# A gated linear attention layer: another order of its small steps, with its operand chains and state stores cut into parts

## The chip, the cores and the metric

The kernel runs on one core of a Trainium2 chip. Its engines work side by side, each through its own list of instructions in order: TensorE (PE, matrix products, with its weight loads listed as PEld), VectorE (DVE), ScalarE (ACT), GpSimd (POOL) and SyncE (SP, which here issues loads from memory). They wait for each other at semaphores. The metric is the device time of one execution in microseconds (us), the median of several runs.

## The reference

One inference step of a four-layer decoder, for one prompt of 256 rows and eight samples of 4 rows, with the same weights; the model width is 1024. The layers mix tokens by pooling, by windowed attention, by gated linear attention and by pooling again, and each is followed by a convolutional feed-forward part. The change touches the third layer's mixer alone. Per head (4 heads, keys of 128, values of 256) it computes

```python
log_a = log_sigmoid(gd @ w_gate_up + b_gate) / 16        # a gate for every key dimension
b = cumsum(log_a)                                        # within a chunk
o_inter = (q * exp(b)) @ S                               # what the state holds
att[t, s] = sum_k q[t, k] * k[s, k] * exp(b[t, k] - b[s, k])   # s <= t
o = o_inter + att @ v
S_new = exp(b_end) * S + (k * exp(b_end - b)).T @ v
o = rms_norm(o) * norm_gain
out = (o * silu(r)) @ w_out
```

The prompt begins with a state of zero; each sample brings a state of 4 x 128 x 256 and hands back a new one.

## The kernel before

**Products in parts.** Every large product is made of three products of rounded parts. A weight piece (4 blocks of 128 rows by 256 columns) is loaded to `raw`, ScalarE writes its rounded part `whi` (L345), VectorE the remainder `wlo` (L353), and `prod` (L414 to L416) sums high by high, high by low and low by high in PSUM. Pieces are split up to four ahead of their use. Six `raw` buffers hold loaded units (1 MB each); SP issues the loads in order (L324), each once its buffer is free.

**The order is written by hand.** `gla_steps` makes a dictionary of named steps and `GLA_ORDER` lists their names; the program is recorded in that order, so the list sets the order on every engine. A name such as `q1c` is a quarter of a projection (12 products for `q`, `k`, `r`, 16 row products for `v`); `w0a` is half of a quarter of the output product (24 products), and a `+` inserts a unit of the next layers' adaLN product (L534). The small steps between them are:

- `ga0` to `ga2`: the gates of a row tile. A product to PSUM (L1605), minimum and difference on VectorE (L1608, L1609), exponential and logarithm on ScalarE, a difference on POOL (L1612). `cu0` to `cu3`: the running sum of a head, as a product with a triangle (L1619, L1620).
- Attention inside a chunk of 128 rows is built in seven levels (halves of 64, 32, ... 1 rows) and a diagonal. `x`, `e` and `z` of a level make its operands: differences of `b` on POOL (L1652, L1653), the exponential on ScalarE (L1657), products with `k` and `q` on VectorE (L1659, L1660). `m0a`, `m0b` and so on multiply them on TensorE for the two row tiles (L1670) and put the result under a mask into `PT0`, `PT1` on VectorE (L1640). `xs5`, `xs6`, `ms5` to `ms7` do the same for the samples (`PTs`).
- `v0` to `v3`: values as rows. The last quarter also evacuates them: ScalarE copies, then a sum `vt` (L809) and a remainder `vs` (L1780) on VectorE.
- `ea`, `eb`, `ec`: the prompt's `K` and `Q` with their decay to the chunk's end; `es` the same for the samples; `ks`, `ps`: key rows and padded attention of the samples. `cr`, `kr`, `op`: attention across the two chunks, transposed keys, the prompt's output of a head.
- For the samples' states, per head: `up` pads the queries on POOL (`qp`, L1818, L1822), `kk` makes masked keys on POOL (`kp`, L1826; one buffer), `uo` multiplies the old state (L1838, L1840), `un` in four parts makes the new state (L1848, and L1851 on VectorE, in the `raw` buffer), whose last part also issues the store (L1854) from POOL. `sp0`, `sp1`: the prompt's new state (L1810, copied by L1811).
- `nq`, `ns`, `nr`, `nm`: squares, sums, roots and scaling of the norm; `og`: times the gate `r` (POOL, L1909), then rounded part and remainder (`gh`, `gl` for heads 0 and 1, `hh`, `hl` for heads 2 and 3).

**Buffers.** Results of the small products share two PSUM buffers (`aux`, tag `aux`) in turn: a product waits until the copy from the one before the last has ended. The projections have four (`mm`), one more (`acc`) holds sums. In SBUF the operands `X` of a level share two buffers (tag `D`), every third has its own (tag `K`).

## Time and profile before

| what | value |
|---|---|
| median of 3 runs | 1399.58 us (1395.9 to 1400.92) |
| the profiled execution | 1404.07 us, its span 1402.3 us |
| mean granted TensorE clock in it | 0.972 |
| TensorE busy | 1337.8 us (95% of the span) |
| VectorE, ScalarE, POOL busy | 850.7, 639.8, 200.2 us |
| gated layer's mixer, first projection to output product | 717.79 to 881.98 us from the span's start |

A row of the timeline gives the start, the duration, the engine, the line, the operation, the output and inputs with their sizes, and in brackets how long the engine had been idle and what ended that. Rows of waits give the waiting engine with its line, what it waited for, the total, the number of times and the longest. Rows of stretches give the busy time of each engine, the granted clock (1.00 is full speed) and the share of the DMA engines. A matrix product on 32-bit data that is not rounded has two records, so eight records are four products.

### The profile page before, as it was taken

The numbers are of one execution on the slowest core, as the hardware profiler recorded it, in microseconds if no ns is written. First come the engines' busy times: TensorE is split into PE (matmuls) and PEld (weight loads), VectorE is DVE, ScalarE is ACT, GpSimd is POOL, SyncE is SP. The second block draws the span as 40 slices with busy tenths as digits, with TensorE's granted clock in tenths as the row PEclk, the third lists the DMA queues.
The fourth block names the chain that finished last, engine by engine and source line by source line (L and its number), as shares of the span: only waits on it lengthen the run. The fifth ranks groups of instructions, "written<-read, shape, count | busy, mean of one in ns | idle before, by whom it ended". The sixth has DMA issues, their size and how long they took to land.

```text
span 1402.3 us, 25413 instructions
## 1 busy us (share of the span) xinstructions
PE 1337.8 (95%) x10075; PEld 1207.1 (86%) x10075; DVE 850.7 (61%) x1674; ACT 639.8 (46%) x1154; POOL 200.2 (14%) x501
## 2 busy tenths in 40 slices
PE   5899999999999999999998988999999999999998
PEld 2478889998887799899978875889999977999997
DVE  3476566556445776665565646586666466777654
ACT  3264344435434464444354435264444345545542
POOL 2211000002001111211033423031010021101100
PEclk9799999999999999999999998999999998999998
DMA  9997788658644787996493244797764576545520
GB/s 350 339 306 272 244 290 299 200 175 286 205 158 152 258 276 274 385 337 203 145 310 118 91 148 155 259 291 257 247 225 161 174 255 215 182 156 164 174 85 34
DMA packets 206231, 310.48 MB, mean 221 GB/s; under 512 B 7692, under 2 KB 186742, under 8 KB 196496
## 3 DMA queue, kind: packets, MB, share of 16 engines
q1 hardware_dynamic: 201296, 286.82, 61.2%
q0 software_dynamic: 4352, 21.50, 4.0%
q8 instruction: 79, 1.29, 0.4%
q10 hardware_dynamic: 464, 0.54, 0.1%
q14 instruction: 40, 0.33, 0.1%
HBM read 300.21 MB, written 19.76 MB: 228 GB/s over the span
## 4 chain that ended last, share of the span: by engine, by line
PE 84%; DVE 8%; ACT 3%; DMA 2%; issue 1%; POOL 1%; SPq 0%; DVEq 0%; ACTq 0%; POOLq 0%
PE mm L414 23%; PE mm L416 22%; PE mm L415 22%; PE adaps L534 4%; PE ps L410 2%; DVE ht L674 1%; DVE hl L710 1%; DVE wlo L353 1%; DMA own<-x_prompt 1%; PE mm L796 1%; PE sqps L596 1%; DMA raw<-w_ada 1%; PE mm L798 1%; PE mm L797 1%; ACT whi L345 1%
## 5 line engine op out<-in xcount | busy, mean ns | idle before, releaser
L414 PE MATMUL mm<-hh,whi 128*128 128x288 f32 x1720 | 517.8, 301 | 4.7 <-ACT hh L705 3.1
L416 PE MATMUL mm<-hh,wlo 128*128 128x288 f32 x1720 | 511.9, 298 | 2.7 <-DVE wlo L353 2.7
L415 PE MATMUL mm<-hl,whi 128*128 128x288 f32 x1720 | 512.5, 298 | 1.9 <-DVE hl L710 1.7
L345 ACT ACTIVATE whi<-raw 128x1024 fp32r<-128x1024 f32 (+2 forms) x335 | 342.7, 1029 | 308.8 <-PE mm L415 230.0
L353 DVE TENSOR_TENSOR wlo<-raw,whi 128x1024 fp32r<-128x1024 f32 (+2 forms) x335 | 394.7, 1195 | 145.2 <-ACT whi L345 144.9
L414 PEld LDWEIGHTS mm<-hh,whi 128*128 128x128 f32 x1720 | 326.5, 190 | 22.7 <-issue 11.2
L415 PEld LDWEIGHTS mm<-hl,whi 128*128 128x128 f32 x1720 | 326.6, 190 | 4.3 <-POOL hs L678 1.7
L416 PEld LDWEIGHTS mm<-hh,wlo 128*128 128x128 f32 x1720 | 326.4, 190 | 3.9 <-DVE wlo L353 3.6
L414 PE MATMUL mm<-ah,whi 128*128 128x288 f32 x704 | 208.5, 296 | 0.0
L416 PE MATMUL mm<-ah,wlo 128*128 128x288 f32 x704 | 208.0, 295 | 0.0
L415 PE MATMUL mm<-al,whi 128*128 128x288 f32 x704 | 206.9, 294 | 0.0
L415 PEld LDWEIGHTS mm<-al,whi 128*128 128x128 f32 x704 | 132.8, 189 | 0.0
L414 PEld LDWEIGHTS mm<-ah,whi 128*128 128x128 f32 x704 | 132.5, 188 | 0.0
L416 PEld LDWEIGHTS mm<-ah,wlo 128*128 128x128 f32 x704 | 132.3, 188 | 0.0
L853 DVE TENSOR_SCALAR c<-ext,vec 128x304 f32<-128x304 f32 x88 | 38.4, 436 | 122.7 <-ACT ext L850 120.2
L856 DVE SCALAR_TENSOR_TENSOR c<-ext,vec,c 128x304 f32<-128x304 f32 x176 | 94.4, 536 | 6.3
L534 PE MATMUL adaps<-raw,cT 128*32 128x512 f32 x736 | 94.2, 642 | 3.3 <-DMA raw<-w_ada 3.3
L862 POOL COPY convS<-ext 128x2 f32<-128x2 f32 x88 | 16.2, 184 | 470.4 <-ACT ext L849 470.3
L849 ACT ACTIVATE ext<-mm 128x256 f32<-128x256 f32 x88 | 33.9, 385 | 86.0 <-PE mm L416 85.9
L872 DVE TENSOR_TENSOR a<-ge,mm 128x256 f32<-128x256 f32 x88 | 36.7, 417 | 49.9 <-PE mm L416 46.4
L534 PEld LDWEIGHTS adaps<-raw,cT 128*32 128x32 f32 x736 | 21.0, 114 | 52.8 <-issue 40.5
L859 ACT ACTIVATE ge<-c 128x304 f32<-128x304 f32 x88 | 39.9, 458 | 56.8 <-DVE c L856 56.7
(394 smaller groups left out, 1502.7 us busy)
## 6 DMA issues: line engine op xcount, KB each, us to landing
raw<-w_ada SPq DMA_DIRECT2D x92, 1024.0 KB, 6.2
raw<-ffn_w_in SPq DMA_DIRECT2D x80, 1024.0 KB, 6.5
raw<-ffn_w_down SPq DMA_DIRECT2D x32, 1024.0 KB, 5.1
raw<-ffn_w_down SPq DMA_DIRECT2D x16, 768.0 KB, 4.2
raw<-gla_w_in SPq DMA_DIRECT2D x12, 1024.0 KB, 12.4
raw<-ffn_w_in SPq DMA_DIRECT2D x16, 512.0 KB, 5.2
win_s<-cache_win_g POOLq DMA_DIRECT2D x16, 512.0 KB, 7.1
raw<-attn_w_in SPq DMA_DIRECT2D x7, 1024.0 KB, 12.7
```

Source lines behind the costliest of these rows:

```text
L345: self.nc.scalar.activation(out=hv, in_=r, func=AF.Copy)
L353: self.nc.vector.tensor_tensor(out=lv, in0=r, in1=hv.bitcast(F32), op=ALU.subtract)
L410: self.nc.tensor.transpose(out=out, in_=in_, identity=self.ident[0:k, 0:k])
L414: mmul(out=out, lhsT=wh, rhs=xh, start=start, stop=False)
L415: mmul(out=out, lhsT=wh, rhs=xl, start=False, stop=False)
L416: mmul(out=out, lhsT=wl, rhs=xh, start=False, stop=stop)
L534: nc.tensor.matmul(out=ps[32 * q:32 * q + 32, :], lhsT=self.cT[:, k * per + r, :], rhs=v[:, r, j * 512:(j + 1) * 512], start=(k == 0), sto ...
L849: nc.scalar.activation(out=e[:, 2:258], in_=ps[t][:, 0:TP], func=AF.Copy)
L853: nc.vector.tensor_scalar(out=c1, in0=e[:, 0:304], scalar1=w[0], scalar2=self.vcol("ffn_conv_b", l * 22 + f), op0=ALU.mult, op1=ALU.add)
L856: nc.vector.scalar_tensor_tensor(out=c1, in0=e[:, k:k + 304], scalar=w[k], in1=c1, op0=ALU.mult, op1=ALU.add)
L859: nc.scalar.activation(out=ge, in_=c1, func=AF.Gelu)
L872: nc.vector.tensor_tensor(out=a[:, 0:TP], in0=ge[:, 0:TP], in1=ps[t][:, 0:TP], op=ALU.mult)
```

## The change

The order of the layer's steps is a new list. For it some steps are cut in parts: the samples' operand chain of both levels runs in three parts (`xa` differences, `xb` exponentials, `xc` products), the samples' end factors too (`sa`, `sb`, `sc`); the stores of the states are steps of their own (`gs0` to `gs3` for the samples, `gp` for the prompt). The padded attention of the samples is laid out with 132 columns per head, so that one instruction fills all heads. Nothing in the mathematics changes.

```diff
 GLA_ORDER = """
-begin + + + + q0a q0b gd q0c q0d masks q1a ga2 q1b ga0 q1c ga1 q1d k0a k0b cu0 k0c k0d cu3 k1a k1b cu2 k1c cu1 k1d
-x0 xs6 xs5 v0a x1 e0 v0b ms5 e1 z0 v0c x2 z1 m0a v0d e2 es m0b v1a z2 x3 m1a v1b e3 m1b ms6 v1c z3 x4 m2a v1d e4 m2b ks
-v2a z4 x5 m3a v2b e5 m3b ms7 v2c z5 x6 m4a ps v2d e6 m4b up0 kk0 v3a z6 m5a uo0 v3b m5b un0a ea v3c eb m6a un0b v3d ec m6b un0c
-r0a m7a un0d up1 kk1 r0b m7b uo1 r0c cr un1a r0d kr0 un1b op1 r1a kr1 un1c op0 r1b op3 un1d up2 kk2 r1c op2 uo2 r1d un2a un2b up3
-r2a uo3 un2c r2b os un2d kk3 r2c nq0 r2d ns0 nq1 r3a ns1 nr0 nq2 un3a r3b ns2 nq3 nm0 r3c ns3 nr1 nm1 og0 un3b r3d og1 nm2 nm3
-og2 og3 un3c un3d sp0 sp1 pre + + w0a w1a w0b w1b w2a w2b w3a w3b end
+begin + + + + q0a q0b gd q0c masks q0d ga2 q1a ga0 q1b ga1 q1c q1d k0a cu0 k0b cu3 k0c cu2 k0d cu1 k1a x0 xa k1b e0 xb k1c x1 sa k1d e1
+v0a z0 x2 v0b xc ms7 e2 v0c z1 m0a v0d ms5 m0b x3 v1a z2 m1a v1b m1b x4 e3 v1c ms6 m2a sb v1d m2b x5 z3 e4
+v2a m3a sc v2b m3b x6 z4 v2c m4a e5 ks v2d m4b ps z5 up0 v3a m5a e6 kk0 v3b m5b ea z6 uo0 v3c m6a un0a v3d m6b eb un0b
+r0a m7a un0c ec up1 r0b m7b un0d kk1 gs0 r0c cr uo1 r0d kr0 un1a up2 r1a kr1 un1b op0 r1b un1c op1 r1c un1d op2 kk2 gs1 r1d uo2 op3 up3
+r2a un2a uo3 r2b os un2b sp0 r2c nq0 un2c sp1 r2d ns0 nq1 un2d kk3 gs2 gp r3a ns1 nr0 nq2 un3a r3b ns2 nq3 nm0 un3b
+r3c ns3 nr1 nm1 og0 un3c r3d og1 nm2 w0a og2 nm3 un3d gs3 w1a og3 pre + + w0b w1b w2a w2b w3a w3b end
 """
...
-        def ends_s():
+        def ends_s(part):
             pl = z["p"]
-            K = z["Ke"] = pl.tile([128, NS], F32, name="Ke")
             bs = z["bs"].rearrange("p (m t) -> p m t", t=4)
...
+            if part == 0:
+                K = z["Ke"] = pl.tile([128, NS], F32, name="Ke")
+                nc.gpsimd.tensor_tensor(out=K.rearrange("p (m t) -> p m t", t=4), in0=bs[:, :, 3:4].broadcast_to([128, 32, 4]),
+                                        in1=bs, op=ALU.subtract)
+            elif part == 1:
+                nc.scalar.activation(out=z["Ke"], in_=z["Ke"], func=AF.Exp)
...
+            else:
+                for e, t in (("Ke", "ks"), ("Qe", "qs")):
+                    nc.vector.tensor_tensor(out=z[e], in0=z[e], in1=z[t], op=ALU.mult)
...
         def pad_s():
 
-            P = z["PTp"] = z["p"].tile([96, H, NB, H, TS], F32R, tag="gd", name="PTp")
+            n = 128 + TS
+            P = z["PTp"] = z["p"].tile([96, H * n], F32R, tag="gd", name="PTp")
             nc.gpsimd.memset(P.bitcast(F32), 0.0)
-            for h in range(H):
-                src = z["PTs"][:, h, :].rearrange("p (b t) -> p b t", t=TS)
-                nc.gpsimd.tensor_copy(out=P[0:32, h, :, h, :], in_=src)
-                nc.gpsimd.tensor_copy(out=P[32:64, h, :, h, :], in_=src)
-                nc.gpsimd.tensor_tensor(out=P[64:96, h, :, h, :], in0=src, in1=P[0:32, h, :, h, :].bitcast(F32), op=ALU.subtract)
+            d = P.rearrange("p (h c) -> p h c", c=n)[:, :, 0:128].rearrange("p h (b g t) -> p h b g t", g=H, t=TS)[:, :, :, 0, :]
+            src = z["PTs"].rearrange("p h (b t) -> p h b t", t=TS)
+            nc.gpsimd.tensor_copy(out=d[0:32], in_=src)
+            nc.gpsimd.tensor_copy(out=d[32:64], in_=src)
+            nc.gpsimd.tensor_tensor(out=d[64:96], in0=src, in1=d[0:32].bitcast(F32), op=ALU.subtract)
...
-            if a == 1:
-                nc.gpsimd.dma_start(out=O["gla_p"][j, 0].rearrange("h k v -> k h v"), in_=z["sp"])
+
+        def s_store():
+            nc.gpsimd.dma_start(out=O["gla_p"][j, 0].rearrange("h k v -> k h v"), in_=z["sp"])
...
-            if a == 3:
-                nc.gpsimd.dma_start(out=O["gla_s"][j, :, h].rearrange("b k v -> k b v"), in_=v)
+
+        def state_store(h):
+            nc.gpsimd.dma_start(out=O["gla_s"][j, :, h].rearrange("b k v -> k b v"), in_=z["S", h])
...
-            if li < LEV:
-                T[f"xs{li}"] = F(level, li, "s")
             T[f"ms{li}"] = F(level_mm_s, li)
+        for k in range(3):
+            T["x" + "abc"[k]] = Step(lambda k=k: [level(li, "s", k) for li in (LEV - 2, LEV - 1)])
```

The lines behind the changed places are up to seven further down in the changed kernel (L1838 is L1843 there, L1851 is L1856, L1909 is L1915).

How this moves instructions, first on VectorE at the gates; `la` and `ga` are the gates' steps, `wlo` a weight remainder. Before:

```order
L1579 CAST mask<-mf 128x1024
L353 TENSOR_TENSOR wlo<-raw,whi 128x1024
L1608 TENSOR_SCALAR la<-ps 32x512
L1609 SCALAR_TENSOR_TENSOR ga<-la,ps 32x512
L1608 TENSOR_SCALAR la<-ps 128x512
L1609 SCALAR_TENSOR_TENSOR ga<-la,ps 128x512
L353 TENSOR_TENSOR wlo<-raw,whi 128x1024
L1608 TENSOR_SCALAR la<-ps 128x512
L1609 SCALAR_TENSOR_TENSOR ga<-la,ps 128x512
L353 TENSOR_TENSOR wlo<-raw,whi 128x1024
```

and now:

```order
L1579 CAST mask<-mf 128x1024
L1608 TENSOR_SCALAR la<-ps 32x512
L1609 SCALAR_TENSOR_TENSOR ga<-la,ps 32x512
L353 TENSOR_TENSOR wlo<-raw,whi 128x1024
L1608 TENSOR_SCALAR la<-ps 128x512
L1609 SCALAR_TENSOR_TENSOR ga<-la,ps 128x512
L1608 TENSOR_SCALAR la<-ps 128x512
L1609 SCALAR_TENSOR_TENSOR ga<-la,ps 128x512
L353 TENSOR_TENSOR wlo<-raw,whi 128x1024 x2
L1623 COPY bs<-ps 128x32 x2
```

The two steps of each gate now stand ahead of the remainders that stood before or between them.

On VectorE again, around the operands of levels 3 and 4; `X` are level operands (64x8 is level 3, 128x4 level 4), `PT` the masked puts, `vt` and `vs` the value evacuation. Before:

```order
L353 TENSOR_TENSOR wlo<-raw,whi 128x1024
L1659 TENSOR_TENSOR X<-X,kf 128x64x8
L1660 TENSOR_TENSOR X<-X,qf 128x64x8
L1640 COPY_PREDICATED PT_7791<-mask,ps 128x4x4x16
L809 TENSOR_TENSOR vt<-mm,vt 32x256
L1780 TENSOR_TENSOR vs<-vt,vs 32x256
L1640 COPY_PREDICATED PT_7792<-mask,ps 128x16x16
L1742 TENSOR_TENSOR Ks<-ps,Ks 32x512
L353 TENSOR_TENSOR wlo<-raw,whi 128x1024
L1659 TENSOR_TENSOR X<-X,kf 128x128x4
L1660 TENSOR_TENSOR X<-X,qf 128x128x4
```

and now:

```order
L809 TENSOR_TENSOR vt<-mm,vt 32x256
L1784 TENSOR_TENSOR vs<-vt,vs 32x256
L1640 COPY_PREDICATED PT_7792<-mask,ps 128x16x16
L1659 TENSOR_TENSOR X<-X,kf 128x64x8
L1660 TENSOR_TENSOR X<-X,qf 128x64x8
L353 TENSOR_TENSOR wlo<-raw,whi 128x1024
L1640 COPY_PREDICATED PT_7791<-mask,ps 128x4x8x8
L1718 TENSOR_TENSOR Ke<-Ke,ks 128x128
L1718 TENSOR_TENSOR Qe<-Qe,qs 128x128
L1640 COPY_PREDICATED PT_7792<-mask,ps 128x32x8
L1659 TENSOR_TENSOR X<-X,kf 128x128x4
L1660 TENSOR_TENSOR X<-X,qf 128x128x4
```

The operands of level 3 stood ahead of the first put of level 2; now they stand behind the value evacuation and the second put of level 2, and those of level 4 behind both puts of level 3.

And on VectorE at the end, from the second root's scaling on; `o<-o,vec,ps` is the scaling of the norm, `gl` and `hl` the remainders of the gated output, `raw` a state update, `sp` the copy of the prompt's state, `rt` the first step of the output product's residual. Before:

```order
L1894 SCALAR_TENSOR_TENSOR o<-o,vec,ps 128x288 x2
L1911 TENSOR_TENSOR gl<-o,gh 128x288 x2
L1851 SCALAR_TENSOR_TENSOR raw<-raw,es,ps 128x256 x2
L1911 TENSOR_TENSOR gl<-o,gh 128x288 x2
L1894 SCALAR_TENSOR_TENSOR o<-o,vec,ps 128x288 x4
L1911 TENSOR_TENSOR hl<-o,hh 128x288 x2
L1909 TENSOR_TENSOR o<-o,r 128x288
L1911 TENSOR_TENSOR hl<-o,hh 128x288 x2
L1851 SCALAR_TENSOR_TENSOR raw<-raw,es,ps 128x256 x4
L1811 COPY sp<-ps 128x512 x2
L353 TENSOR_TENSOR wlo<-raw,whi 128x1024 x2
L622 TENSOR_TENSOR rt<-mm,modT_103 128x32
```

and now:

```order
L1900 SCALAR_TENSOR_TENSOR o<-o,vec,ps 128x288 x2
L1917 TENSOR_TENSOR gl<-o,gh 128x288 x2
L1856 SCALAR_TENSOR_TENSOR raw<-raw,es,ps 128x256 x2
L1917 TENSOR_TENSOR gl<-o,gh 128x288 x2
L1900 SCALAR_TENSOR_TENSOR o<-o,vec,ps 128x288 x2
L353 TENSOR_TENSOR wlo<-raw,whi 128x1024
L1917 TENSOR_TENSOR hl<-o,hh 128x288 x2
L1900 SCALAR_TENSOR_TENSOR o<-o,vec,ps 128x288 x2
L1856 SCALAR_TENSOR_TENSOR raw<-raw,es,ps 128x256 x2
L353 TENSOR_TENSOR wlo<-raw,whi 128x1024
L1915 TENSOR_TENSOR o<-o,r 128x288
L1917 TENSOR_TENSOR hl<-o,hh 128x288 x2
```

The copies of the prompt's state are gone from here: they now stand among the states of head 2, ahead of the roots. The last state update stood ahead of the prompt's state and behind all gating; now it is ahead of the last head's gating, and the remainders of weights, for the output product, stand between.

## The prediction

> **What bounds the kernel now.** I read the page's busy times first, then busy time by stretch of the gated layer, then who waited for whom on TensorE, then the granted clock in two-microsecond stretches, and last the order of time at the places where a wait ends.

> The page's first part, and busy time by stretch of the gated layer (columns: stretch, its length, then busy time and instructions of PE, PE's weight loads, DVE, ACT and POOL, then the granted clock, the DMA share and GB/s). The stretches are: query, key and gate projections; the seven levels with the value projection; heads and states; gating and prompt state, up to the output product; the output product. (The norm, left out, has no wait.)

> ```profile
> PE 1337.8 (95%) x10075; PEld 1207.1 (86%) x10075; DVE 850.7 (61%) x1674; ACT 639.8 (46%) x1154; POOL 200.2 (14%) x501
> ...
> 717.79:755.93 38.14, 36.55 (x235) 31.92 (x236) 20.05 (x29) 20.75 (x39) 8.77 (x13) 0.96 0.78 249
> 755.93:810.20 54.27, 48.43 (x421) 46.61 (x420) 37.31 (x56) 26.39 (x47) 26.68 (x37) 0.97 0.26 78
> 810.20:847.20 37.00, 31.86 (x258) 28.58 (x257) 18.30 (x35) 13.35 (x21) 8.33 (x13) 1.00 0.52 176
> ...
> 864.02:881.98 17.96, 11.13 (x42) 6.77 (x41) 11.92 (x23) 5.88 (x12) 6.05 (x8) 0.71 0.25 87
> 881.98:908.00 26.02, 26.02 (x200) 26.00 (x196) 14.31 (x38) 9.53 (x14) 0.21 (x5) 1.00 0.77 280
> ```

> TensorE sets the time of the kernel as a whole (95%). In the gated layer it does not: from 717.79 to 881.98 it is idle for about 19.5 us, and in the stretch before the output product the clock is 0.71. A rearrangement of this layer can win that idle time and slow clock, and nothing else. TensorE's waits from 690 to 915 us (total, times, longest) name their ends:

> ```profile
> PE ps L1810 <- DVE raw L1851: 3.4, 1, 3.4
> PE ps L1681 <- DVE PT L1640: 3.2, 2, 2.2
> PE ps L1891 <- DVE raw L1851: 2.0, 1, 2.0
> PE acc L1838 <- POOL qp L1822: 2.0, 1, 2.0
> PE ps L1670 <- DVE PT L1640: 1.7, 1, 1.7
> PE ps L1681 <- ACT X L1657: 1.6, 1, 1.6
> PE ps L1619 <- POOL la L1612: 1.6, 1, 1.6
> PE ps L1848 <- DVE o L1894: 1.2, 2, 0.8
> PE ps L1670 <- DVE X L1660: 1.0, 1, 1.0
> PE ps L1798 <- DVE raw L1851: 1.0, 1, 1.0
> PE ps L1798 <- ACT Kt L1732: 0.5, 1, 0.5
> PE ps L1891 <- DVE o L1894: 0.3, 1, 0.3
> ```

> By stage: gates 1.6; levels 3.2 + 1.7 + 1.6 + 1.0 = 7.5; heads and states 2.0 + 1.0 + 0.5 = 3.5; the end 3.4 + 2.0 + 1.2 + 0.3 = 6.9. Sum 19.5.

> Behind three of these waits TensorE is busy without a pause, but at a lower clock (same columns as above):

> ```profile
> 742.00:744.00 2.00, 2.00 (x14) 2.00 (x13) 1.40 (x3) 1.12 (x2) 0.00 (x0) 0.72 0.12 25
> 744.00:746.00 2.00, 2.00 (x10) 2.00 (x10) 0.38 (x1) 0.00 (x0) 0.00 (x0) 0.50 0.93 309
> 746.00:748.00 2.00, 2.00 (x15) 1.84 (x15) 0.12 (x1) 1.48 (x6) 0.00 (x0) 0.93 0.58 199
> 790.00:792.00 2.00, 2.00 (x13) 1.99 (x14) 2.00 (x4) 0.00 (x0) 1.94 (x2) 0.66 0.89 308
> 792.00:794.00 2.00, 2.00 (x12) 1.96 (x11) 0.57 (x1) 0.00 (x0) 1.72 (x6) 0.50 0.00 0
> 874.00:876.00 2.00, 2.00 (x6) 1.55 (x6) 0.36 (x1) 0.73 (x1) 0.93 (x1) 0.50 0.00 0
> 876.00:878.00 2.00, 2.00 (x6) 1.62 (x5) 0.55 (x1) 0.00 (x0) 0.00 (x0) 0.50 0.91 319
> 878.00:880.00 2.00, 2.00 (x7) 1.43 (x5) 0.15 (x1) 0.00 (x0) 0.00 (x0) 0.65 0.59 205
> ```

> Time lost to the clock is stretch times (1 - clock): 2 x (0.28 + 0.50 + 0.07) = 1.7 us behind the gates' wait, 2 x (0.34 + 0.50) = 1.7 behind a level's wait, 2 x (0.50 + 0.50 + 0.35) = 2.7 in the prompt state's products. Together 6.1, so 25.6 us are there to be won. [...]

> **The change, part by part.** The matrix products stay the same in number and shape, so TensorE's own work does not change; what changes is who is late.

> *Gates.* In order of time:

> ```profile
> 733.03 1.12 PE L1605 MATMUL ps<-wg,gd 17*128 17x512 f32 x2
> 735.24 1.48 DVE L353 TENSOR_TENSOR wlo<-raw,whi 128x1024 fp32r<-128x1024 f32 x1 [2.40 <-ACT whi L345]
> 736.64 0.68 DVE L1608 TENSOR_SCALAR la<-ps 128x512 f32<-128x512 f32 x1
> 739.61 1.27 POOL L1612 TENSOR_TENSOR la<-la,ga 128x512 f32<-128x512 f32 x1 [3.98 <-ACT ga L1611]
> 740.93 0.49 PE L1619 MATMUL ps<-cm,la 128*128 128x128 f32 x2 [1.59 <-POOL la L1612]
> ```

> The last gate's product ends at 734.15, but its first VectorE step starts at 736.64, behind a weight remainder (`wlo`) that waits for ScalarE. Now that remainder stands behind the gate's two steps, so the chain can begin about 2.4 us earlier; the cumulative product still comes 36 products later. 1.6 + 1.7 (clock) = +3.3. If the chain gains only half (another delay on ScalarE, whose copy `whi` is now between the gates' exponentials), some 0.4 us of waiting stays; that is the lower end.

> *Levels.* The first two waits (1.6 for the samples' exponentials, 1.0 for level 0) go: the samples' last level, which needs no exponential, comes first, and 16 row products more stand before level 5 of the samples. The waits for `PT` (3.2 + 1.7) come from level products that need one of the two `aux` buffers while VectorE is behind; pairing is different now, and those go as well. But the operands of levels 3 to 6 (`z3` to `z6`) are now multiplied behind the second product of the level before, and VectorE has the value evacuation ahead of them. The prices, from the first value projection and from the level operations:

> ```profile
> 767.66 1.00 PE L1670 MATMUL ps<-X 128*128 128x64 f32 x8
> 769.34 0.78 DVE L1780 TENSOR_TENSOR vs<-vt,vs 32x256 fp32r<-32x256 f32 x1 [0.48 <-ACT vs L1778]
> 770.44 1.00 PE L1670 MATMUL ps<-X 128*128 128x64 f32 x8
> ...
> L1660 DVE TENSOR_TENSOR X<-X,qf x7: 674/680/1527, 764.0 to 802.1; 128x512 f32<-128x512 f32 x7
> ...
> L1640 DVE COPY_PREDICATED PT<-mask,ps x16: 420/445/744, 766.9 to 817.6; 128x256 f32<-128x256 uint8 x14, 128x512 f32<-128x512 uint8 x2
> ```

> Level products come every 770.44 - 767.66 = 2.78 us. From the start of the product that follows a finished value unit, VectorE ends `vs` at 770.12 - 767.66 = 2.46, then puts the mask (0.45) and makes the two operands (0.68 each, begun 0.6 apart: 1.3): 4.2, so the next level's product, due at 2.78, waits 1.4 to 1.5. This holds for level 3 and level 5. With one 1.53 for 0.68 (row L1660, its longest) it is 2.3. I take 1.6 and 1.5. Level 4 has no evacuation ahead: product 0.85, put 0.45, operands 1.3 make 2.6, or 3.5 with one long one, against 2.78: 0 to 0.7, taken 0.5. Level 6 has a state product (1.2 us) in between: 0. The unmasked product waits for a buffer behind `vs` again (0.3), the cross product behind `K` and `Q` (0.4). New waits 4.3, between 3.2 and 6. Net: 7.5 + 1.7 - 4.3 = +4.9.

> *Heads and states.* The store of head 0 made POOL wait and held back the query pad of head 1:

> ```profile
> 817.08 0.98 POOL L1854 DMA_DIRECT2D gla_s<-raw  x1 [11.05 <-DVE raw L1851]
> ```

> Now pad and keys are made first and the store is issued behind them. 2.0 goes; the waits for `raw` and `Kt` (1.5) lose their cause mostly, since both row transposes come before the first head's output; I keep 0.6 for copies from PSUM between neighbours in `aux`. +2.9. Fewer POOL steps for the sample pad (3 for 12) are worth nothing by themselves: POOL is 14% busy, and the pad is ready early.

> *The end.* The prompt state's products move from behind the gating, where they waited 3.4 and ran at half clock, to a place among the projections of head 2, where TensorE is warm. The output product of heads 0 and 1 begins before heads 2 and 3 are gated: 2 x 24 products, which took 26.02 / 200 = 0.13 us each in the output stretch, so 6.2 us of work, plus adaLN products, lie beside the last gating. All four waits (6.9) and the clock (2.7) go. What can be late instead is head 3: from the third normalization on, TensorE has 6.2 + 0.7 + 0.3 + 1.9 = 9.1 us of work, and 1.6 more before the product that needs head 3. The chain needs about 11.4 (VectorE in order: 2.0 to head 2's scaling, POOL 2 x 1.0, copy and remainder 1.0, head 3's scaling 1.0, a state update 0.9, a remainder 1.2, POOL 1.9 with the store ahead, copies and remainders 1.3). 0.7, and 0.3 for a square behind the root: -1.0. If the chain is 3 us longer, 4 us. +8.6. POOL's price is this row, the store's share is the 0.98 above:

> ```profile
> L1909 POOL TENSOR_TENSOR o<-o,r 128x288 f32<-128x288 f32 x7 | 7.0, 1015 | 12.2 <-DVE o L1894 12.2
> ```

> *Clock behind the new waits.* Two of the six waits between 1.6 and 2.2 us were followed by a slow stretch of 1.7; with two new waits of 1.5 I charge one: -1.7, bounds 0 and -5.

> Sum: 3.3 + 4.9 + 2.9 + 8.6 - 1.7 = 18.0 us. The profiled execution took 1404.07 us (span 1402.3), 4.5 above the median; the layer's waits belong to the program, so 18.0 comes off the median: 1399.6 - 18.0 = 1381.6.

> **The rivals.** *Level products bound by VectorE.* Each of levels 3 to 6 waits for its operands beside a POOL step: 2.3 + 1.6 + 2.3 + 1.5, three slow stretches in place of one: 7.7 - 3.6 + 3.4 = 7.5 less, 1389.1. For it: the 1.53 beside a POOL step, and that the change issues the next POOL step just ahead of each pair. Against it: 6 of 7 pairs ran at 0.68. [...]

> *The end stays late.* Head 3's chain is 3 us longer, and the output product then starts at half clock: 3 + 2.7 = 5.7 less, 1387.3. For it: VectorE was busy 11.92 of 17.96 us there. Against: 48 products now cover it.

> *Given back to the weight loads.* TensorE reaches the adaLN products earlier and waits there for transfers: gain at most 7, 1393 to 1399. For it: the output stretch moves 280 GB/s. Against: its TensorE is busy 26.02 of 26.02.

> *Slower: late stores block the load queue.* SP issues loads in order, and loads into a state's buffer wait for its store:

> ```profile
> SPq L324 <- DMA gla_s<-raw: 29.2, 3, 10.9
> gla_s<-raw POOLq DMA_DIRECT2D x4, 1024.0 KB, 5.8
> ```

> The last store now stands behind six gating steps, and adaLN loads stand behind it. By my count the load behind head 2's store lands about 6 us before it is needed; beyond that each microsecond of delay is one lost, and the change is slower by over 0.5% once that store is 18 + 7 + 6 = 31 us late. At 33 us the time is 1381.6 + 27 = 1408.6. Against it: the longest such wait of the load queue was 10.9, and the state updates ahead of the stores now end earlier.

> **How the numbers follow.** Forecast 0.62 (own range 1376 to 1387), level rival 0.14, late end 0.10, given back 0.10, late stores 0.04. The range leaves out the last two and a tail below: 1375.5 to 1392. About 0.5% (7.0 us) is what a measurement of this kernel can tell from no change. Faster: the first three, 0.86; same 0.10; slower 0.04.

> **What would show it.** Gates: no wait of L1619's counterpart, clock 1.00 behind it. Levels: the level products wait for VectorE's `X` operands, about 1.5 us twice, and no longer for `PT`. States: no wait for `qp`. The end: the prompt state's products at a clock near 1.00; waits, if any, of the output product's second half for `hh` or `hl`. I am wrong if the sum of TensorE's waits in the layer stays above 12 us, if level 3 to 6 wait over 2 us each, or if a wait for a transfer appears behind the output product.

## The result

| | before | changed |
|---|---|---|
| median | 1396.39 us (1392.94 to 1405.20, 20 runs) | 1386.3 us (1381.76 to 1399.55, 20 runs) |
| profiled execution | 1404.07 us, span 1402.3 | 1381.93 us, span 1380.1 |

The ratio is 0.9921, with a 95% interval of 0.9902 to 0.9940: the change makes the kernel about 11 us faster, where 18.0 had been forecast. That is outside the 0.5% that counts as no change, and the forecast of 1381.6 is 4.7 us too low. The gain came out 7 to 8 us smaller than forecast; that the kernel before took 1396.4 and not 1399.6 us in these runs makes up for 3.2 of it. Two single executions of 2141 us at a granted clock of 0.557, one of the kernel before and one of "operands ahead" below, are in none of the ratios.

The profiled spans differ by 22.2 us, twice the timed gain, so a span must not be read as the gain. The copy of the first small projection (`gd`, L1589), ahead of every moved step, starts at 722.90 us in the trace before and at 711.17 in the one after: 11.7 us of the difference lie there, where both kernels execute the same steps. The granted clock up to that copy is 0.97 in the trace before and 0.99 in the one after. This differs from execution to execution and is not the change: in the ten experiments below, which are the same up to that point as well, the copy starts anywhere from 710.5 to 723.1, and two that keep most of the change (prompt state back, updates back) start it at 722.7 and 722.9. All that follows is therefore read from that copy on, to the first adaLN product (L534) behind the output product. TensorE has the same products in between; I call that length the layer. The rows are busy time by stretch (columns as in the prediction), cut at two points with the same products done on both sides: the first value projection, and the place where both the cross product and the second head's product with its old state are done. Before:

```profile
722.90:755.77 32.87, 31.28 (x197) 27.59 (x196) 15.58 (x20) 16.75 (x33) 4.58 (x4) 0.95 0.73 236
755.77:823.15 67.38, 57.82 (x500) 55.00 (x499) 45.62 (x70) 29.50 (x51) 31.15 (x42) 0.97 0.30 94
823.15:908.15 85.00, 76.68 (x511) 65.13 (x510) 46.48 (x98) 37.32 (x62) 15.72 (x23) 0.94 0.57 198
```

and after:

```profile
711.17:740.98 29.81, 29.74 (x197) 26.05 (x196) 14.97 (x20) 17.78 (x36) 9.41 (x11) 1.00 0.78 247
740.98:808.76 67.78, 60.24 (x500) 55.40 (x499) 49.09 (x73) 28.66 (x49) 26.89 (x29) 0.96 0.29 90
808.76:886.04 77.28, 74.71 (x509) 63.34 (x509) 47.44 (x95) 36.72 (x61) 16.00 (x20) 1.00 0.66 228
```

The layer went from 185.25 to 174.87 us, 10.4 shorter, which agrees with the timed 11. By stage: gates 3.1 shorter; levels and cross product 0.4 **longer**; heads and end 7.7 shorter. The gain that is missing is in the middle stage, where the clock is 0.96, no better than the 0.97 before.

TensorE's waits from 690 to 915 us in the changed kernel (total, times, longest):

```profile
PE ps L1670 <- DVE X L1660: 4.4, 3, 1.7
PE ps L1723 <- DVE PT L1640: 1.9, 1, 1.9
PE ps L1670 <- DVE PT L1640: 1.1, 2, 0.8
PE ps L410 <- DVE raw L1856: 0.8, 1, 0.8
...
PE ps L1814 <- DVE o L1872: 0.4, 1, 0.4
...
PE mm L414 <- ACT hh L1916: 0.4, 1, 0.4
PE ps L1802 <- ACT Kt L1735: 0.4, 1, 0.4
...
PE ps L1897 <- DVE o L1900: 0.3, 1, 0.3
```

These add up to 9.7 us, where the layer had 19.5. The waits for the gates (`la`), for the query pad (`qp`) and the three long ones of the end are gone. Of what is left, 7.4 us are in the level stage: the level products wait for their operands (`X`), the cross product (L1723) for the put of the diagonal, two products of the diagonal and of a level for a buffer.

Behind two of these waits the clock is low:

```profile
768.00:772.00 4.00, 4.00 (x23) 3.91 (x23) 1.06 (x4) 0.44 (x1) 0.00 (x0) 0.57 0.65 190
...
805.00:810.00 5.00, 4.71 (x32) 3.25 (x33) 2.83 (x8) 0.60 (x1) 1.63 (x4) 0.66 0.44 156
```

The first is behind the wait of level 3, the second behind that of the cross product: 4 x 0.43 = 1.7 and 5 x 0.34 = 1.7 us lost.

What makes the two longest of the waits that had not been foreseen at their size is seen in the order of time. At level 4, of all engines' rows those of POOL, VectorE's operands and the product that waits:

```profile
772.78 1.04 POOL L1652 TENSOR_TENSOR X<-bf 128x512 f32<-128x512 f32 x1 [6.83 <-PE ps L1670]
...
773.02 1.34 DVE L1659 TENSOR_TENSOR X<-X,kf 128x512 f32<-128x512 f32 x1
...
773.78 1.49 POOL L1653 TENSOR_TENSOR X<-bf 128x512 f32<-128x512 f32 x1
...
774.29 1.52 DVE L1660 TENSOR_TENSOR X<-X,qf 128x512 f32<-128x512 f32 x1
...
775.96 0.41 PE L1670 MATMUL ps<-X 128*128 128x64 f32 x2 [1.38 <-DVE X L1660]
```

POOL makes the differences of level 6 at the same time, and the two operand products take 1.34 and 1.52 us, where the same step alone takes 0.68. At the cross product:

```profile
801.85 2.10 POOL L1831 TENSOR_TENSOR kp<-Ks,bcol 96x1024 fp32r<-96x1024 f32 x1 [11.35 <-PE ps L1853]
...
802.12 2.39 DVE L1701 TENSOR_TENSOR Q<-Q,qf 128x512 f32<-128x512 f32 x1
...
804.43 0.71 DVE L1640 COPY_PREDICATED PT<-mask,ps 128x512 f32<-128x512 uint8 x1
...
805.29 0.91 PE L1723 MATMUL ps<-Q,K 128*128 128x128 f32 x6 [1.92 <-DVE PT L1640]
```

POOL's masked keys of head 1 (`kk1`, L1831) start in front of VectorE's query product, which then takes 2.39 us; the put of the diagonal behind it ends at 805.14, and the cross product waits until then.

### The profile page after: what moved, and what is told of

Read it like the earlier page. It is cut to its first block, busy times and chain, and to the rows that moved or that the text cites. A ratio compares the mean times of both kernels' runs of the same rounds, so it can differ in the third digit from the quotient of the medians.

```text
span 1380.1 us, 25398 instructions
## 1 busy us (share of the span) xinstructions
PE 1323.0 (96%) x10075; PEld 1195.4 (87%) x10075; DVE 854.4 (62%) x1674; ACT 639.0 (46%) x1154; POOL 203.2 (15%) x492
## 4 chain that ended last, share of the span: by engine, by line
PE 82%; DVE 8%; ACT 4%; DMA 2%; POOL 1%; issue 1%; SPq 1%; DVEq 0%; POOLq 0%; ACTq 0%
PE mm L414 22%; PE mm L416 22%; PE mm L415 22%; PE adaps L534 4%; PE ps L410 2%; DVE ht L674 2%; DVE hl L710 1%; DMA raw<-w_ada 1%; DVE wlo L353 1%; SPq L324 1%; DMA own<-x_sample 1%; PE sqps L596 1%; PE mm L796 1%; PE ps L1670 1%; PE mm L798 1%
## 5 line engine op out<-in xcount | busy, mean ns | idle before, releaser
L414 PE MATMUL mm<-hh,whi 128*128 128x288 f32 x1720 | 514.5, 299 | 5.1 <-ACT hh L705 3.1
L353 DVE TENSOR_TENSOR wlo<-raw,whi 128x1024 fp32r<-128x1024 f32 (+2 forms) x335 | 395.9, 1199 | 138.2 <-ACT whi L345 137.8
L345 ACT ACTIVATE whi<-raw 128x1024 fp32r<-128x1024 f32 (+2 forms) x335 | 342.7, 1029 | 298.8 <-PE mm L415 213.8
L414 PEld LDWEIGHTS mm<-hh,whi 128*128 128x128 f32 x1720 | 323.1, 188 | 23.1 <-issue 9.9
L415 PEld LDWEIGHTS mm<-hl,whi 128*128 128x128 f32 x1720 | 323.0, 188 | 4.8 <-POOL hs L678 2.1
L416 PEld LDWEIGHTS mm<-hh,wlo 128*128 128x128 f32 x1720 | 322.9, 188 | 4.0 <-DVE wlo L353 3.7
L414 PE MATMUL mm<-ah,whi 128*128 128x288 f32 x704 | 208.5, 296 | 0.0
L414 PEld LDWEIGHTS mm<-ah,whi 128*128 128x128 f32 x704 | 132.5, 188 | 0.0
L534 PE MATMUL adaps<-raw,cT 128*32 128x512 f32 x736 | 91.4, 625 | 5.3 <-DMA raw<-w_ada 5.3
L534 PEld LDWEIGHTS adaps<-raw,cT 128*32 128x32 f32 x736 | 20.6, 112 | 51.9 <-issue 39.3
## 6 DMA issues: line engine op xcount, KB each, us to landing
raw<-w_ada SPq DMA_DIRECT2D x92, 1024.0 KB, 7.3
raw<-ffn_w_in SPq DMA_DIRECT2D x80, 1024.0 KB, 6.8
raw<-ffn_w_down SPq DMA_DIRECT2D x32, 1024.0 KB, 5.1
raw<-gla_w_in SPq DMA_DIRECT2D x12, 1024.0 KB, 11.4
raw<-attn_w_in SPq DMA_DIRECT2D x7, 1024.0 KB, 12.0
```

Source lines behind the costliest of these rows:

```text
L345: self.nc.scalar.activation(out=hv, in_=r, func=AF.Copy)
L353: self.nc.vector.tensor_tensor(out=lv, in0=r, in1=hv.bitcast(F32), op=ALU.subtract)
L414: mmul(out=out, lhsT=wh, rhs=xh, start=start, stop=False)
L415: mmul(out=out, lhsT=wh, rhs=xl, start=False, stop=False)
L416: mmul(out=out, lhsT=wl, rhs=xh, start=False, stop=stop)
L534: nc.tensor.matmul(out=ps[32 * q:32 * q + 32, :], lhsT=self.cT[:, k * per + r, :], rhs=v[:, r, j * 512:(j + 1) * 512], start=(k == 0), sto ...
```

## The experiments

All of them rewrite the list of steps only; the computation stays whole. Their diffs show the parts of the lines that change, and `...` stands for lines left out. The table gives the layer's length (from the copy L1589 to the first L534 product behind the output product, in one profiled execution each) and the time against the kernel before, which was timed anew beside them (medians 1397.7 to 1398.3 us).

| run | layer, us | against the change | ratio to before, 95% interval |
|---|---|---|---|
| before | 185.25 | +10.4 | 1 |
| the change | 174.87 | 0 | 0.9921 (0.9902 to 0.9940) |
| keys later | 171.64 | -3.2 | 0.9882 (0.9833 to 0.9930) |
| operands ahead | 167.91 | -7.0 | 0.9887 (0.9827 to 0.9946) |
| new gates and levels, old rest | 183.46 | +8.6 | 0.9996 (0.9962 to 1.0029) |
| old gates and levels, new rest | 177.56 | +2.7 | 0.9939 (0.9908 to 0.9969) |
| prompt state back | 173.13 | -1.7 | 0.9929 (0.9906 to 0.9952) |
| output product back | 178.36 | +3.5 | 0.9937 (0.9914 to 0.9960) |
| updates back | 176.14 | +1.3 | 0.9973 (0.9944 to 1.0002) |
| keys, operands and kr0 | 167.47 | -7.4 | 0.9870 (0.9836 to 0.9904) |
| keys, operands, prompt state | 162.86 | -12.0 | 0.9822 (0.9787 to 0.9857) |
| the same, kr0 and pads between | 162.98 | -11.9 | 0.9849 (0.9810 to 0.9887) |

The layer's length is the finer measure: what agrees in it agrees to some tenths, and with one exception (updates back) the times go with it within their intervals.

**The two halves of the change.** First the new list up to the cross product with the old one behind it (the other pieces of the change, such as the stores as steps of their own, are in both):

```diff
 un0d kk1 gs0 r0c cr uo1
-r0d kr0 un1a up2 r1a kr1 un1b op0 r1b un1c op1
+un1a r0d kr0 un1b op1 r1a kr1 un1c op0 r1b op3
...
```

> The new order up to the cross product, and behind it the old order of heads, states, norm, prompt state and output product. By the prediction's terms (gates 3.3, levels 4.9 less 1.7 for clock, query pad 2.0) it is 8.5 us faster than the kernel before. By the stage lengths in the two traces (gates 3.1 shorter, levels and cross product 0.4 longer) it is 2.7 us faster: the gain of the level stage was eaten up by its new waits.

that is, the new list's part ahead of the cut and the old list's behind it; and the reverse, with the old part ahead of the cut:

```diff
...
-un0d kk1 gs0 r0c cr uo1
+un0d gs0 up1 kk1 r0b m7b uo1 r0c cr
 r0d kr0 un1a up2 r1a kr1 un1b op0 r1b un1c op1
```

> The other half: the old order up to the cross product, behind it the new order of heads, states, norm, prompt state and output product. By the prediction's terms (end 8.6, waits of heads 0.9) it is 9.5 us faster than the kernel before; by the stage lengths in the two traces 7.7. If the two halves do not depend on each other, this gain and that of the other half add up to the 10 to 11 us of the whole change.

The first half is worth 1.8 us by the layer and 0.6 by the time (interval -4.0 to 5.3), so the 8.5 of the prediction's terms is out, and the 2.7 of the stage lengths is near. (The layer contains one wait of 2.7 us that is in neither list, see below; without it the first half would be worth 4.5 at most.) The second half is worth 7.7 by the layer and 8.5 by the time. Together 9.5 of 10.4: the halves hardly depend on each other. Waits of the first half:

```profile
PE ps L1670 <- DVE X L1660: 4.4, 3, 1.7
PE ps L1814 <- DVE raw L1856: 3.4, 1, 3.4
PE ps L1853 <- DVE raw L1856: 2.7, 1, 2.7
PE ps L1897 <- DVE raw L1856: 2.0, 1, 2.0
PE ps L1723 <- DVE PT L1640: 1.9, 1, 1.9
```

The waits of the changed level stage are all there, and the two longest of the old end (3.4 and 2.0) come back. The 2.7 belongs to the seam between the two lists: the old list's first state updates follow at once there. In the second half:

```profile
PE ps L1681 <- DVE PT L1640: 3.1, 2, 2.2
PE ps L1670 <- DVE X L1660: 2.7, 1, 2.7
PE acc L1843 <- POOL qp L1827: 2.0, 1, 2.0
PE ps L1670 <- DVE PT L1640: 1.7, 1, 1.7
PE ps L1619 <- POOL la L1612: 1.6, 1, 1.6
```

The old gates and levels wait as they did; the 2.7 stands for 1.6 and 1.0 there, since the samples' chains run in the three parts of the change here. The three long waits of the old end are not among this run's waits; the fourth, 0.3 us, is in both kernels.

**Keys later.** Is it POOL that makes the cross product late, or the place of the put behind `K` and `Q`?

```diff
-r0b m7b un0d kk1 gs0 r0c cr
+r0b m7b un0d gs0 kk1 r0c cr
```

> The changed kernel with one step moved: POOL makes the masked keys of head 1 (L1831) behind the store of head 0 and no longer ahead of it. Theory (POOL and a two-input VectorE step get in each other's way): in the changed kernel the query product L1701 took 2.39 us beside this POOL step, which held back the put of the diagonal and so the cross product, which waited 1.93 us and ran at half clock behind it. Now L1701 takes about 0.7, the wait of L1723 falls below 0.5, the slow stretch (1.7 us lost) goes, and the kernel is 3 us faster than the changed one. Rival (the put is late because K and Q stand ahead of it on VectorE, whatever POOL does): L1701 or the put stay late, the wait of L1723 stays above 1.4, and the time stays within 1 us.

In the order of time:

```profile
801.46 0.68 DVE L1701 TENSOR_TENSOR Q<-Q,qf 128x512 f32<-128x512 f32 x1
802.06 0.72 DVE L1640 COPY_PREDICATED PT<-mask,ps 128x512 f32<-128x512 uint8 x1
...
802.92 1.13 PE L1723 MATMUL ps<-Q,K 128*128 128x128 f32 x8 [0.23 <-DVE PT L1640]
```

The query product takes 0.68 for 2.39, the wait is 0.23 for 1.92, the slow stretch is gone, and the layer is 3.2 us shorter where 3 had been expected. VectorE's order did not change. POOL was the cause. (The masked keys now stand beside the four scalings of `K`, L1727, one of which takes 2.49 us there; in this place TensorE waits only 0.2 us for them.)

**Operands ahead.** Do levels 3 to 5 wait for the place of their operands, or has VectorE too much to do, so that the waits would only change their name?

```diff
-v1c ms6 m2a sb v1d m2b x5 z3 e4
-v2a m3a sc v2b m3b x6 z4 v2c m4a e5 ks v2d m4b ps z5 up0 v3a m5a e6 kk0 v3b m5b ea z6 uo0
+v1c ms6 z3 m2a e4 sb v1d m2b x5
+v2a m3a sc e5 z4 v2b m3b x6 v2c m4a z5 ks e6 v2d m4b ps up0 v3a m5a z6 kk0 v3b m5b ea uo0
```

> The changed kernel with the operand products of levels 3 to 6 and their exponentials each moved ahead by one or two steps, so that they no longer stand behind the second put of the level before. Theory (their place alone makes level products 3 to 5 wait): the waits of L1670 for X, 4.4 us in the changed kernel, fall below 1, the slow stretch behind level 3 (1.8 us lost) goes, and the kernel is 5 to 6 us faster than the changed one. Rival (VectorE has too much to do in these stages): the waits come back as waits for PT, more than 3 us of them, and the time gains less than 1.5 us.

The longest waits that are left:

```profile
PE ps L1723 <- DVE PT L1640: 1.9, 1, 1.9
PE ps L1670 <- DVE PT L1640: 1.1, 2, 0.8
PE ps L410 <- DVE raw L1856: 0.9, 1, 0.9
```

The row of L1670 for `X` is not there any more, that for `PT` is the 1.1 of the change: nothing came back under another name. The layer is 7.0 us shorter, 4.4 of waits and 1.7 of clock among it. POOL still takes its part, at level 3:

```profile
761.22 2.25 POOL L1653 TENSOR_TENSOR X<-bf 128x512 f32<-128x512 f32 x1
...
762.55 1.47 DVE L1659 TENSOR_TENSOR X<-X,kf 128x512 f32<-128x512 f32 x1
```

Here an operand takes 1.47 beside POOL, and nobody waits, since it is made two products earlier (those of levels 4 and 5 one product earlier). POOL's order is the same in both kernels, so the place decides whether there is a wait; that POOL adds to its length is read from the durations. How much of the 4.4 either would be alone was not tried.

**What made the end shorter.** The end had three moves in one: the prompt state's products (`sp`) go forward, the last sample updates (`un3c`, `un3d`) go ahead of the last gating, and half of the output product begins before heads 2 and 3 are gated. Each was put back. First the prompt state:

```diff
-un2b sp0 r2c nq0 un2c sp1 r2d ns0 nq1 un2d kk3 gs2 gp r3a
+un2b r2c nq0 un2c r2d ns0 nq1 un2d kk3 gs2 r3a
...
-w1a og3 pre + + w0b
+w1a og3 sp0 sp1 gp pre + + w0b
```

> The changed kernel with only the prompt state's products (sp0, sp1) and their store put back behind all gating; the last sample update and the early half of the output product stay where the change has them. In the kernel before, the first of these products waited 3.4 us for a sample update and all ran at half clock (2.7 us lost). Theory (that wait hung on VectorE doing the update behind the gating, and this update is now done ahead of it): no wait over 1 us comes back, the clock stays near 1.00, and the layer is within 1 us of the changed kernel's 174.8 us. Rival, by the prediction's terms (the early place of the prompt state is what wins): 3.4 + 2.7 = 6.1 us come back.

There is no wait ahead of these products, and they run at full speed (sixteen, with their durations in ns; most took 630 in the kernel before):

```profile
L1814 PE MATMUL ps<-v,Kt x16: 379/379/380, 870.7 to 873.9; 128*128 128x256 f32 x16
```

The layer even is 1.7 us shorter than the change's: behind the gating these 3.5 us of products cover head 3's chain, for which the output product's second half waits in the changed kernel (the row of L414 for `hh` above, 0.4, is gone, and the 48 products of the second half take 6.5 us for 7.5). The 0.4 that the first of them waited for `o` at the early place (L1814) is gone too. The early place of the prompt state was not what won. Next the output product:

```diff
-nm2 w0a og2 nm3 un3d gs3 w1a og3 pre + + w0b w1b
+nm2 og2 nm3 un3d gs3 og3 pre + + w0a w1a w0b w1b
```

> The changed kernel with only the early half of the output product (w0a, w1a) put back behind the gating. Theory (what it does is to stand between small products that share two PSUM buffers, TensorE's work up to the second half being the same in either order): the last normalization's product waits about 1.9 us for a copy and the last sample update's product about 0.9, the wait for hh (0.4) goes, and the layer is 2 to 3 us longer than the changed kernel's 174.8. Rival, by the prediction's working (these 48 products cover the last gating): the four waits of the end, 6.9 us less the prompt state's 3.4, come back as 3.5 us or more, with a slow stretch.

Of the waits the two that come back, and the clock behind them:

```profile
PE ps L1897 <- DVE raw L1856: 2.0, 1, 2.0
...
PE ps L1853 <- DVE o L1900: 0.4, 1, 0.4
```

```profile
861.00:868.00 7.00, 6.32 (x23) 2.29 (x24) 5.28 (x13) 1.33 (x3) 2.56 (x4) 0.53 0.20 47
```

The waits are the 1.9 and, half as long, the 0.9 of the theory, but the slow stretch (7 x 0.47 = 3.3 us, at most, since TensorE is idle for 0.7 of it), which only the rival had, comes with them. The output product's two halves take 1.4 us less here, and with that set against the rest the layer is 3.5 us longer. Neither account holds whole: the waits that come back add up to 2.4 us, nearer the theory's 2.8 than the rival's 3.5, but the slow stretch is the rival's. Last, the prompt state and the updates together:

```diff
-og0 un3c r3d og1 nm2 w0a og2 nm3 un3d gs3 w1a og3 pre
+og0 r3d og1 nm2 w0a og2 nm3 w1a og3 un3c un3d gs3 sp0 sp1 gp pre
```

> The changed kernel with the prompt state's products and the last two sample updates (un3c, un3d) put back behind all gating, the early half of the output product still ahead. Theory (VectorE's order, the update behind the gating, makes the prompt state wait): its first product waits 2 to 3 us for raw though 48 products stand ahead of it, and the layer is 2 to 5 us longer than 174.8, the upper end if the products then run at half clock. Rival (the cover by the 48 products is enough): no wait over 1 us, layer within 1 us.

```profile
PE ps L1814 <- DVE raw L1856: 2.9, 1, 2.9
```

The old wait is back at 2.9 for 3.4, in front of the same products that waited for nothing in the run with the prompt state alone put back. Against that run the layer is 3.0 us longer; against the change 1.3, less than expected, as the 1.7 is in it. The clock stays at 1.00 here. The time says more (0.9973) than the layer (9.1 us of 1396 would be 0.9935); that stays open.

**A version that beats both.** Three moves together: the operands as in "operands ahead", the keys, and kr0, the first transposes of the prompt's keys:

```diff
-un0d kk1 gs0 r0c cr uo1 r0d kr0 un1a
+un0d gs0 kk1 r0c cr uo1 kr0 r0d un1a
```

> The changed kernel with three moves at once: level operands ahead as tried, the masked keys of head 1 behind the store as tried, and the first transposes of the prompt's keys (kr0) ahead of the last part of the first gate projection, so that their copy does not stand behind that part's evacuation on ScalarE. By the layer lengths in the traces (174.8 changed, 3.2 less with the keys moved, 6.9 less with the operands) and 0.8 for the second transposes' wait the layer is 163.9 us long, and the kernel is 10.9 us faster than the changed one and 21 to 22 faster than the one before. If the moves get in each other's way (other waits for PT), it is less than 8 us faster than the changed one.

The layer is 7.4 us shorter than the change's, below the bound that had been set for "they get in each other's way". The miss of 3.5 has one place, a wait of 1.8 us with a slow stretch behind it (granted clock 0.57 from 801 to 805 us, 4 x 0.43 = 1.7):

```profile
797.81 2.74 DVE L1727 TENSOR_SCALAR K<-K,ep 128x128 f32<-128x128 f32 x3
798.04 1.91 POOL L1831 TENSOR_TENSOR kp<-Ks,bcol 96x1024 fp32r<-96x1024 f32 x1
...
800.35 0.33 PE L410 MATMUL ps<-cm,K 128*128 128x128 f32 x1 [1.76 <-DVE K L1727]
```

The masked keys, moved away from the query product, now run beside the four scalings of `K`, and kr0, moved ahead, needs these. With kr0 left in its place there are products of the projection to cover it. So the next run leaves kr0 alone and puts the prompt state back:

```diff
-un0d gs0 kk1 r0c cr uo1 kr0 r0d un1a
+un0d gs0 kk1 r0c cr uo1 r0d kr0 un1a
...
-un2b sp0 r2c nq0 un2c sp1 r2d
+un2b r2c nq0 un2c r2d
...
-w1a og3 pre
+w1a og3 sp0 sp1 gp pre
```

> The changed kernel with three moves: level operands ahead, masked keys of head 1 behind the store, and the prompt state's products behind the gating; the transposes kr0 stay where the change has them. By the layer lengths (6.9, 3.2 and 1.7 us shorter one by one) the layer is 163.0 us long against the changed kernel's 174.8, and the kernel takes about 1374.5 us. If the early products of the prompt state hid something that only shows in this order, a wait over 1 us comes up among the last heads and the layer stays above 165.

The layer is 162.86 us against 163.0 expected, and the median 1375.74 us (1372.84 to 1380.03): the three gains add up. Its longest waits:

```profile
PE ps L1670 <- DVE PT L1640: 1.1, 2, 0.8
...
PE ps L1802 <- ACT Kt L1735: 0.4, 1, 0.4
PE ps L410 <- DVE raw L1856: 0.3, 1, 0.3
```

No wait of 1 us is left, and the clock is 1.00 over the whole layer:

```profile
717.89:880.75 162.86, 160.16 (x1203) 142.18 (x1201) 110.51 (x187) 83.21 (x145) 52.16 (x59) 1.00 0.58 191
```

The last run moves kr0 again and keeps POOL busy with a query pad until the scalings are over:

```diff
-un0d gs0 kk1 r0c cr uo1 r0d kr0 un1a up2 r1a
+un0d gs0 up2 kk1 r0c cr uo1 kr0 r0d un1a r1a
```

> As the run before, with kr0 moved ahead again, and the query pad of head 2 (three short POOL steps, 1.0 us) put between the store and the masked keys of head 1. Theory (with the keys right behind the store, POOL's product L1831 ran beside VectorE's four scalings of K, L1727, which took 2.94 us for 0.89, and this made kr0 wait 1.75 us): the scalings are over before L1831 begins and take about 0.9 again, kr0 waits less than 0.4, and the layer is 0.5 to 1 us shorter than in the run before, about 162.3. Rival (the scalings are late for their place behind a weight remainder): kr0 waits 1 us or more.

```profile
L1727 DVE TENSOR_SCALAR K<-K,ep x4: 269/290/431, 803.9 to 804.6; 128x128 f32<-128x128 f32 x4
```

```profile
PE ps L1853 <- DVE raw L1856: 0.6, 1, 0.6
```

The scalings are short (0.29 in the middle, 0.43 at most), and kr0 does not wait, as the theory has it; but a state update waits 0.6 in its place, and the layer has the length of the run before (162.98). The 0.5 to 1 us did not come.

## Why the prediction was right or wrong

**Direction, place and kind of the gains: right.** The chance of 0.86 for faster went the right way, and the views it rested on (waits of TensorE, granted clock behind them) name the places that changed.

**Gates, forecast +3.3: 3.1.** The wait for `la` is gone and the clock is 1.00 in that stage, both in the change and in the run that has only the new gates and levels; with the old gates (old gates and levels, new rest) the 1.6 is back. No run undid the gates' moves one by one.

**Levels, with the query pad and the clock behind new waits (4.9 + 2.0 - 1.7 = +5.2): -0.4. This is the step that failed.** What goes was right: 9.5 us of waits and 1.7 of clock are not there any more. What comes was sized too low, three terms of it:

- The sum of new waits was 4.3, measured 7.4. Level 3 (1.6) and level 5 (1.5) were right: 1.71 and 1.34. Level 4 was taken at 0.5 with 0.7 as its upper end, by allowing one operand product of 1.53: both were slow (1.34 and 1.52), and the wait is 1.38. The cross product was taken at 0.4 and waited 1.92, because the step that the list moved next to it, POOL's masked keys, was not counted as something that could slow VectorE; moving it away gives 3.2 us back. The puts' buffer waits were taken at 0.3 and are 1.1.
- The clock behind new waits was charged once (1.7) and comes twice (3.4). The reading behind the charge was off as well: the wait of 2.0 for `raw` at L1891 was also followed by a slow stretch (granted clock 0.58 from 869 to 870 us, before the wait of 3.4 began at 870.2), so it was three of the six waits and not two.
- The remaining 0.8 us or so of that stage are in no row of a wait.

Four places of the list gave this back, and putting them right (operands ahead, keys later) returned 10.2 us by the sum of the two runs. So the level rival had one part, at 1389.1 (VectorE's steps longer beside POOL's, 1.34 to 2.39 us for 0.68), and the forecast's own count had the other part (operands behind the second put). It was wrong to make one of them the forecast and the other a rival, since a list can do both, at different levels.

**Heads and end (0.9 + 8.6 = +9.5): 7.7.** The three long waits of the end, 6.6 of its 6.9 us, and the half clock go. The remaining waits there add up to 2.3, where 1.6 were kept (0.6 for heads, 1.0 for head 3). The 1.0 for head 3 is about right: the second half of the output product takes 1.0 us longer than in the run that covers it. (The terms listed for the chain add up to 11.3, not 11.4.) But the prediction gave the 3.4 us wait and the 2.7 of clock to the early place of the prompt state's products. The runs say that it was the sample updates ahead of the gating on VectorE that took the wait away (3.0 us between two runs that differ in it alone), that the early half of the output product is worth 3.5, waits and clock together, and that the prompt state's early place costs 1.7. Nor did the half clock begin with the prompt state's wait: it began behind the 2.0 at L1891, ahead of the 3.4; it comes back with that 2.0 when the early half is put back, and does not come when the updates are put back and the prompt state waits 2.9. Whether the 3.4 made it last longer stays open.

**The other rivals.** No product of the layer waited for a transfer, and no late store held the loads back far enough for TensorE to notice (the load queue's longest wait for a state's store went from 10.9 to 18.4 us): both stay out. The end did not stay late either: the second half of the output product waits 0.4 for `hh`, at a clock of 1.00. The time fell between the forecast and the level rival.

**The base.** Subtracting from the median of three runs, 1399.6, was a choice with 3 us in it: 20 runs, these three among them, gave 1396.4. It worked against the error in the gain here, by luck.

## What to carry to other kernels

When a hand-written order moves steps, list for each moved step of POOL what VectorE has at that time, and for each moved step of VectorE what POOL has: VectorE's steps took up to nine times as long beside POOL's here (a scaling of `K` 2.49 us for 0.27). Put the operands of a product a whole product ahead of it; then a slow step beside POOL was no wait here (1.47 us for 0.68 at level 3), and 7.0 of the 12.0 us that the best list here wins beyond the change are just that. A gain that two moves share belongs to neither until one of them has been undone: the prompt state's early place, which the forecast paid with 6 us, was a loss.

## What the runs showed of the hardware that had not been expected

**POOL held up VectorE's one-tensor steps too.** The prediction's row was a product of two tensors (0.68, and 1.53 for one beside a POOL step). The scalings of `K` (L1727, one tensor times a scalar for each partition) took 0.27 to 0.30 us each away from POOL (up to 0.43 for one of the four beside a short POOL step of 0.33) and 2.48 to 2.49 for one of them in the three runs that put POOL's masked keys beside them (keys later; keys, operands and kr0; keys, operands, prompt state). In the run of keys, operands and kr0 that scaling ends at 800.29 us, 0.34 behind POOL's step of 1.91 us, and it is recorded as begun before that step (797.81 against 798.04). What in POOL's step holds the scaling up, no run shows.

**Short waits and the clock.** The wait of 1.71 us at level 3 was followed by a slow stretch in all six traces that have it, and so was the wait of 1.92 to 1.93 at the cross product, six times of six; each stretch was 3.4 us long at a granted clock of 0.50 and cost 1.7 us. The waits of 1.33 to 1.38 at levels 4 and 5 never were. But length alone does not decide it: 2.25 (a sample level, old levels with new rest), 2.68 (the seam) and 2.85 (updates back) were followed by a clock of 1.00. Of the 23 waits between 1.59 and 1.99 us in the layers of the twelve traces, outside a stretch that was slow already, 19 were followed by a slow stretch; in this layer such a wait is best priced at twice its length.
